# One inference step of a gMLP and S5 decoder layer: weight pairs loaded earlier in the startup, and a ring of two tiles for the last products

## The chip, the cores and the metric

The kernel runs on one core of a Trainium2 chip. The metric is device time in microseconds (us) of one execution. TensorE multiplies matrices (PE, with its weight loads as PEld), VectorE (DVE), ScalarE (ACT) and GpSimd (POOL) do the elementwise work, and SyncE (SP) issues every DMA of this kernel from one queue, in order.

## What is computed

All matrices are fp32. Besides one prompt of 2048 positions there are 8 decode positions, which run through the same matmuls as extra columns.

```python
shift, scale, gate = split(silu(c) @ w_c + b_c, 3)      # adaLN: c is 9 x 2048, w_c 2048 x 6144
h    = rmsnorm(x, g_pre) * (1 + scale) + shift          # x: 2048 x 2048 and 8 x 2048
proj = h @ w_in                                         # w_in: 2048 x 5120
u_a, v_a, z_a, x_b, z_b = split(proj)
y_a  = u_a * chunk_mix(layernorm(v_a)) * silu(z_a)      # 8 heads, chunks of 128 positions
y_b  = s5_branch(x_b) * silu(z_b)                       # 64 groups, a 64-dim complex state each
o    = concat(y_a, y_b) @ w_out                         # w_out: 2048 x 2048
out  = x + gate * rmsnorm(o, g_post)
```

## The kernel before

Activations lie transposed: 128 features on the partitions, positions along the free axis, in four blocks of 512 positions (the last has the 8 decode positions too). The contraction over 2048 features is cut into 16 K tiles of 128. Each fp32 operand is split into a high and a low part (`split`, L87: ACT casts the high part in L90, DVE or POOL subtracts it in L85 to give the low part), and one product of a weight tile and a K tile is three matmuls (`mm3`, L97 to L99). A weight load is a raw tile of 128 x 1024 fp32, 512 KB, issued by `wraw` (L106); `wpieces` turns it into two high and two low pieces.

**Startup** (`startup`, L1237; its instructions keep the order of the code on each engine). It computes the RMS statistic of block 0, the shift and scale of adaLN, and the first six column tiles of the input projection together. After the loads of x come the constants (`constants1`), whose last lines add four slices of the identity into `sel`; then 8 adaLN loads, which are a ring of 8 (`NR_`), then weight pairs of the input projection. A pair is one raw tile for two column tiles and four K tiles; there are two raw buffers for pairs. The loop over `s` runs one K tile a turn: six `kstep`s (18 matmuls) for K tile `s - 2`, four adaLN matmul groups (`ada`, L275; each frees its ring tile and issues the adaLN load 8 further on), the copy of the adaLN result (L279), its transposition through `sel` (`ada_turn`, L286), and from that h for K tile `s - 1` (`hmake`). The pairs that K tiles 4q to 4q+3 need are loaded in the turns `s = 4q` (two) and `s = 4q + 1` (the third), and split in the same two turns.

**Input projection** with everything for the S5 branch, then the **output projection** (`phase3`). In these the library orders each engine's instructions by a timeline that it plans itself: the order of the code is the priority, and an operation may be put earlier when its inputs and its tile are free. In `phase3` each block first runs four column tiles together over the 16 K tiles (six in the last block), then one column tile after the other. Each result is copied to a tile `o` (`ev_o`) and its square is added up. `final` finishes a block while the next one runs: it takes the reciprocal root R, and for each of 16 tiles multiplies `o` by R in place (L1154), adds the residual `xres` in place (L1155, POOL for even tiles and DVE for odd ones), and stores `o` (L1156). `xres` has 4 buffers, `o` has `OB` = 20. The finishing steps are called one at a time (`finish_some`) between matmuls. The last 256 positions are computed with positions on the partitions (`phase3_rows`), with weight loads from `in_woutr` and matmuls L1214 to L1216. `phase3` and `phase3_rows` load and split their first weight pairs at their start.

In `s5_mats` small results are copied from PSUM: L799 on DVE, L853 on DVE and ACT in turn.

Of the kernel before, what the change touches and what calls it, by code (L numbers as in the profile page):

```python
# [21 lines left out]
ND = 8  # L22
T = L + ND
NB = 4
# [20 lines left out]
NW = 5  # L45
OB = 20
LAG = 6
# [15 lines left out]
class Builder:  # L63
# [155 lines left out]
    def constants1(self):  # L219
        c = self.cp  # L220
        def load(name, shape):
            t = c.tile(shape, F32, name="c_" + name)
            self.SP.dma_start(t, self.I[name])
            return t
        self.ident = load("ident", [128, 128])
        self.bcT = load("bcT", [128, 48])
        self.gpre = load("gpre", [128, KT])
        self.gpost = load("gpost", [128, KT])
        self.sel = c.tile([128, 9], F32, name="sel")
        self.V.tensor_add(self.sel, self.ident[:, 0:9], self.ident[:, 32:41])  # L230
        for i in (64, 96):
            self.V.tensor_add(self.sel, self.sel, self.ident[:, i : i + 9])

# [512 lines left out]
    def s5_mats(self, pp, i):  # L746
# [51 lines left out]
        c = tl([128, 2, NQ, 32], "sc")  # L798
        V.tensor_copy(c.rearrange("p r q c -> p (r q c)"), pc[:, 0 : 2 * NQ * 32])  # L799
        dw = tl([32, NQ, 32], "dw")  # L800
# [51 lines left out]
        for g, q, jh in quarters:  # L852
            (S.copy if jh else V.tensor_copy)(kf[:, q, jh * 4 : jh * 4 + 4, :].rearrange("p j c -> p (j c)"), pk[g * 32 : g * 32 + 32, 0:128])  # L853
        V.tensor_add(kf[:, :, 0, :], kf[:, :, 0, :], dw)
# [237 lines left out]
    def phase3(self, b, ws, y):  # L1092

        V, G, SP = self.V, self.G, self.SP
        rs = ranges(b) if b < NB - 1 else ranges(b)[1:]
        c0 = rs[0][0]
        nn = rs[-1][0] + rs[-1][1] - c0
        ng = 4 if b < NB - 1 else 6
        ssq = self.xp.tile([128, TB + ND], F32, tag="ssq", bufs=2, name=self.nm("ossq"))
        kw = [{}, self.wkw]  # L1100
        ws = ws or [self.wgroup(0, 0, ng, *kw)]
        acc = [[self.ps.tile([128, 512], F32, tag="acc" if g < 4 else "aux", bufs=4, name=self.nm("acc"))] for g in range(ng)]
        os_ = []
        for k in range(KT):
            while len(y) < min(KT, k + 6):
                y.append(self.yload(b, len(y)))
            if k in (11, 13, 15):
                self.finish_some(1)
            if k % 4 == 0 and k < KT - 4:
                ws.append(self.wgroup(0, k // 4 + 1, ng, *(kw[::-1] if k // 4 % 2 == 0 else kw)))  # L1110
            for g in range(ng):
                self.kstep(acc[g], ws[k // 4][g], k, y[k], rs, k == 0, k == KT - 1)
        ynext = []
        w = self.wcol(self.I["wout"][ng])
        for g in range(ng):
            self.finish_some(1)
            os_.append(self.ev_o(b, g, acc[g], rs, ssq, G))
        for n in range(ng, 16):
            ac = [self.ps.tile([128, 512], F32, tag="acc", bufs=4, name=self.nm("acc")) for _ in rs]
            nxt = []  # L1120
            for k in range(KT):
                if k % 8 == 0 and n < 15:
                    nxt += self.wsplit(self.whalf(self.I["wout"][n + 1], k // 8), **(self.wkw if k else {}))
                self.kstep(ac, w, k, y[k], rs, k == 0, k == KT - 1)
                if k == 13:
                    self.run_later()
                if n == 15 and b < NB - 1 and k >= 4 and k % 2 == 0:
                    ynext.append(self.yload(b + 1, len(ynext)))
            self.finish_some(1 if n < 15 or b == NB - 1 else 16)
            if b == NB - 1 and n % 2 == 0 and 6 <= n < 14:  # L1130
                self.gg_rows((n - 6) // 2)
            os_.append(self.ev_o(b, n, ac, rs, ssq, G))
            w = nxt
        self.finish_some(16)
        self.finish = self.final(ssq, nn, os_, b * TB + c0, b * TB)
        return y if b == NB - 1 else ynext

    def final(self, ssq, nn, os_, t0, out0):
# [11 lines left out]
        for n in range(16):  # L1150
            if n < 13:
                load()
            o, x = os_[n][:, 0:nn], xs[n]
            V.tensor_mul(o, o, R[:, 0:nn])  # L1154
            (V if n % 2 else G).tensor_tensor(o, o, x, op=ALU.add)  # L1155
            SP.dma_start(self.O["yT"][n * 128 : n * 128 + 128, out0 : out0 + nn], o)  # L1156
            yield 1
# [13 lines left out]

    def phase3_rows(self, b, y):

        V, G, S, T, SP = self.V, self.G, self.S, self.T, self.SP
        ssq = self.sp_.tile([128, 2, 4], F32, name="ssqr")
        src = lambda i: self.I["woutr"][i // 8][:, i % 8 * 2 : i % 8 * 2 + 2, :].rearrange("p k m -> p (k m)")
        kws = [{}, self.wkw]
        ws = {i: self.wsplit(src(i), **kws[i % 2]) for i in range(4)}
        os_, xs = {}, {}
# [20 lines left out]
        for f in range(4):  # L1200
# [3 lines left out]
            for k in range(KT + lag):  # L1204
# [20 lines left out]
                if k < KT and k % 2:  # L1225
                    if i + 4 < 32:
                        ws[i + 4] = self.wsplit(src(i + 4), **kws[i % 2])
                    if f or k >= 13:
                        self.finish_some(1)
                    if f * 16 + k >= XR0 and len(xs) < 8:  # L1230
                        c, g = len(xs) // 4, len(xs) % 4
                        x = self.xp.tile([128, OW], F32, tag="o", bufs=OB, name=self.nm("xr"))[:, 0:512]
                        SP.dma_start(x, self.I["xr"][c][:, g * 512 : g * 512 + 512])
                        xs[c, g] = x


    def startup(self, st, NG, ntl):  # L1237
# [8 lines left out]
        def wraw(g, kq):  # L1246
            pair[g, kq] = self.wraw(self.wpair(I["win"], ntl[1][g], kq), st, "wraw2", 2)
        def wsplit(g, kq):
# [5 lines left out]
        for i in range(NR_):  # L1254
            raw(i)
        wraw(0, 0)
        wraw(2, 0)
        ssq = self.tile_()
        for k in range(KT):
            self.stat_add(st, xs[k], ssq, k, TB, V)  # L1260
        R = self.R[0]
        def ada(ps, i):
            self.ada_mm(ps, raws.pop(i), i % 4)
            raw(i + NR_)
# [10 lines left out]
        wsplit(0, 0)  # L1275
        wraw(4, 0)
        self.ada_ss2(0, sb)
# [9 lines left out]
        for s in range(2, KT + 2):  # L1287
# [6 lines left out]
            for q in range(NG):  # L1294
# [13 lines left out]
                if s < KT:  # L1308
                    if s % 4 == 0 and q in (0, 2):
                        wraw(q, s // 4)  # L1310
                    if s % 4 == 1 and q == 3:
                        wraw(4, s // 4)
                    if (s % 4, q) in ((0, 3), (1, 2), (1, 4)):
# [6 lines left out]
    def build(self):  # L1320
# [129 lines left out]
        self.wkw = {"pool": self.xp, "tags": ("w3h", "w3l"), "bufs": 5}  # L1450
        for b in range(NB):
            if b == NB - 1:
                self.lo_engs = [V, V, V, G]
                self.ggr = []
            y = self.phase3(b, [ws0] if b == 0 else None, y0 if b == 0 else y)
        self.phase3_rows(NB - 1, y)
        self.close(cm_x)
# [73 lines left out]
```

## Time and profile before

| | |
|---|---|
| median of three runs | 2971.8 us (2971.3 to 2975.4) |
| the profiled execution | 2969.24 us, its span 2967.4 us |
| PE busy | 2846.7 us, 96% of the span |
| DVE, ACT, POOL busy | 1590.0, 1059.7, 1046.0 us |
| mean granted TensorE clock | 0.987 of full speed |
| DMA | 581.14 MB, 196 GB/s over the span |

The profiled execution is 2.6 us below the median of the runs, and 1.8 us of it lie outside the span. Two matmuls overlap in the pipeline, so a busy PE can still run at half clock; the granted clock is told by stretch. A wait is put down to the instruction that ended it.

### The profile page before, as it was taken

The numbers are of one execution on the slowest core, as the hardware profiler recorded it, in microseconds if no ns is written. First come the engines' busy times: TensorE is split into PE (matmuls) and PEld (weight loads), VectorE is DVE, ScalarE is ACT, GpSimd is POOL, SyncE is SP. The second block draws the span as 40 slices with busy tenths as digits, with TensorE's granted clock in tenths as the row PEclk, the third lists the DMA queues.
The fourth block names the chain that finished last, engine by engine and source line by source line (L and its number), as shares of the span: only waits on it lengthen the run. The fifth ranks groups of instructions, "written<-read, shape, count | busy, mean of one in ns | idle before, by whom it ended". The sixth has DMA issues, their size and how long they took to land.

```text
span 2967.4 us, 44344 instructions
## 1 busy us (share of the span) xinstructions
PE 2846.7 (96%) x15804; PEld 2387.4 (80%) x15804; DVE 1590.0 (54%) x3026; ACT 1059.7 (36%) x1960; POOL 1046.0 (35%) x971
## 2 busy tenths in 40 slices
PE   5899899999999999999999999999999999999896
PEld 3567677777999999988888888888888878878785
DVE  4347946648543646466546745583641361543755
ACT  3224433433333232333334332433243423434442
POOL 0107735364242232323232223222324353352433
PEclk9999999999999999999999999999999999999998
DMA  8777898997887373856576566646573463564666
GB/s 299 270 201 217 237 258 236 258 270 221 194 205 214 105 232 119 251 163 189 166 215 195 161 193 185 209 132 215 162 217 110 117 206 121 142 213 128 202 199 206
DMA packets 456560, 581.14 MB, mean 196 GB/s; under 512 B 216594, under 2 KB 303122, under 8 KB 456338
## 3 DMA queue, kind: packets, MB, share of 16 engines
q1 hardware_dynamic: 456338, 578.32, 65.3%
q8 instruction: 124, 2.03, 0.3%
q14 instruction: 98, 0.79, 0.1%
HBM read 466.87 MB, written 102.66 MB: 192 GB/s over the span
## 4 chain that ended last, share of the span: by engine, by line
PE 57%; DVE 8%; DMA 3%; issue 2%; ACT 1%; SPq 0%; POOL 0%; DVEq 0%; ACTq 0%; POOLq 0%
PE acc L99 17%; PE acc L97 16%; PE acc L98 16%; DVE Ub L898 2%; DVE o L1154 1%; DVE wlo L85 1%; DMA x<-in_xT 1%; DMA wraw<-in_wout 1%; PE mix L530 1%; PE acc L1214 1%; PE acc L1215 1%; PE acc L1216 1%; DMA wraw<-in_woutr 1%; PE pg L979 1%; DVE sct L908 1%
## 5 line engine op out<-in xcount | busy, mean ns | idle before, releaser
L97 PE MATMUL acc<-hi,whi 128*128 128x512 f32 (+2 forms) x3200 | 1131.4, 355 | 4.0 <-DVE x L374 2.2
L98 PE MATMUL acc<-lo,whi 128*128 128x512 f32 (+2 forms) x3200 | 1122.3, 351 | 2.4 <-DVE lo L85 2.1
L99 PE MATMUL acc<-hi,wlo 128*128 128x512 f32 (+2 forms) x3200 | 1122.0, 351 | 1.9 <-DVE wlo L85 1.6
L85 DVE TENSOR_TENSOR wlo<-wraw,whi 128x512 fp32r<-128x512 f32 x628 | 518.9, 835 | 882.4 <-ACT whi L90 858.5
L90 ACT CAST whi<-wraw 128x512 fp32r<-128x512 f32 x960 | 581.4, 621 | 1142.7 <-PE acc L98 791.0
L85 POOL TENSOR_TENSOR wlo<-wraw,whi 128x512 fp32r<-128x512 f32 x332 | 459.8, 1387 | 1131.8 <-ACT whi L90 1027.3
L97 PEld LDWEIGHTS acc<-hi,whi 128*128 128x128 f32 x3200 | 603.2, 189 | 100.7 <-issue 23.4
L99 PEld LDWEIGHTS acc<-hi,wlo 128*128 128x128 f32 x3200 | 603.6, 189 | 90.7 <-DVE wlo L85 4.7
L98 PEld LDWEIGHTS acc<-lo,whi 128*128 128x128 f32 x3200 | 604.6, 189 | 80.2 <-DVE lo L85 3.9
L99 PE MATMUL acc<-yhi,wlo 128*128 128x512 f32 (+1 forms) x1024 | 379.6, 372 | 16.7 <-DVE wlo L85 15.2
L97 PE MATMUL acc<-yhi,whi 128*128 128x512 f32 (+1 forms) x1024 | 378.6, 370 | 6.4 <-ACT whi L90 3.6
L98 PE MATMUL acc<-ylo,whi 128*128 128x512 f32 (+1 forms) x1024 | 378.3, 370 | 0.0
L99 PEld LDWEIGHTS acc<-yhi,wlo 128*128 128x128 f32 x1024 | 195.3, 191 | 54.5 <-DVE wlo L85 18.0
L97 PEld LDWEIGHTS acc<-yhi,whi 128*128 128x128 f32 x1024 | 195.6, 191 | 42.5 <-ACT whi L90 4.1
L98 PEld LDWEIGHTS acc<-ylo,whi 128*128 128x128 f32 x1024 | 195.4, 191 | 34.0
L898 DVE SCALAR_TENSOR_TENSOR Ub<-Ub,apow 128x128 f32<-128x128 f32 (+6 forms) x384 | 143.3, 440 | 2.5 <-ACT Ub L885 2.2
L987 POOL TENSOR_TENSOR sg<-sg,zbl 128x264 f32<-128x264 f32 x64 | 54.7, 855 | 191.6 <-DVE sg L986 127.8
L1076 POOL TENSOR_TENSOR ossq<-ossq,osq 128x512 f32<-128x512 f32 (+1 forms) x60 | 81.8, 1363 | 47.8 <-ACT osq L1069 47.0
L369 ACT ACTIVATE hi<-x,shiftT 128x512 fp32r<-128x512 f32 x96 | 68.4, 724 | 82.1 <-DVE x L368 78.8
L368 DVE SCALAR_TENSOR_TENSOR x<-x,GT,R 128x512 f32<-128x512 f32 x96 | 82.2, 872 | 23.9 <-DMA x<-in_xT 23.7
L90 ACT CAST hh<-hr 128x264 fp32r<-128x264 f32 x64 | 26.4, 414 | 191.4 <-DMA hr<-Ub 107.3
L342 POOL TENSOR_TENSOR ssq<-ssq,t 128x512 f32<-128x512 f32 (+1 forms) x45 | 60.9, 1353 | 72.7 <-ACT t L341 71.8
(287 smaller groups left out, 2798.5 us busy)
## 6 DMA issues: line engine op xcount, KB each, us to landing
wraw<-in_win SPq DMA_DIRECT2D x320, 512.0 KB
wraw<-in_wout SPq DMA_DIRECT2D x128, 512.0 KB
xr<-XB SPq DMA_DIRECT2D x128, 272.0 KB
x<-in_xT SPq DMA_DIRECT2D x128, 256.0 KB
wraw<-in_wss SPq DMA_DIRECT2D x64, 512.0 KB
XB<-t SPq DMA_DIRECT2D x64, 256.0 KB
wraw<-in_wgt SPq DMA_DIRECT2D x32, 512.0 KB
MQ<-qh SPq DMA_DIRECT2D x128, 128.0 KB
```

Of the source, the lines that this page charges most:

```text
L85: eng.tensor_tensor(out, a, b, op=ALU.subtract)
L90: self.S.copy(hi, raw)
L97: mm(acc, whi, xhi, start=start, stop=False)
L98: mm(acc, whi, xlo, start=False, stop=False)
L99: mm(acc, wlo, xhi, start=False, stop=stop)
L342: add_eng.tensor_tensor(ssq[:, 0:n], ssq[:, 0:n], sq[:, 0:n], op=ALU.add)
L368: V.scalar_tensor_tensor(xt, xt, self.GT[:, k, 0:1], R[:, 0:TB], op0=ALU.mult, op1=ALU.mult)
L369: S.activation(hi[:, 0:TB], xt, AF.Identity, bias=self.shiftT[:, k, 0:1])
L530: T.matmul(pm[:, c * 128 : c * 128 + 128], self.vtok[:, c, hs], self.wsT[:, h, :], start=True, stop=True)
L898: V.scalar_tensor_tensor(o, i, f, o, op0=ALU.mult, op1=ALU.add)
L987: self.G.tensor_tensor(sg, sg, zb, op=ALU.mult)
L1076: eng.tensor_tensor(ssq[:, 0:nn], ssq[:, 0:nn], sq[:, 0:nn], op=ALU.add)
```

## The change

It moves the four-slice sum `sel` from `constants1` to after the statistic of block 0. It gives the weight pairs of the startup three buffers instead of two, issues the first three pairs together, and issues the pairs for K tiles 4q to 4q+3 in turn `s = 4q - 2` instead of `4q` and `4q + 1`. It puts the copies of L799 and L853 on ACT. In `final` the product goes into a new tile `fin` (two buffers), the sum goes into `xres`, and `xres` is stored; `OB` becomes 21. In `phase3` the finishing steps at K tiles 11, 13 and 15 come after the matmuls of that tile, and the first weight pairs of the next block (or the first two row weights) are loaded and split during the last column tile.

```diff
-OB = 20
+OB = 21
...
-        self.sel = c.tile([128, 9], F32, name="sel")
-        self.V.tensor_add(self.sel, self.ident[:, 0:9], self.ident[:, 32:41])
-        for i in (64, 96):
-            self.V.tensor_add(self.sel, self.sel, self.ident[:, i : i + 9])
...
-        V.tensor_copy(c.rearrange("p r q c -> p (r q c)"), pc[:, 0 : 2 * NQ * 32])
+        S.copy(c.rearrange("p r q c -> p (r q c)"), pc[:, 0 : 2 * NQ * 32])
...
-            (S.copy if jh else V.tensor_copy)(kf[:, q, jh * 4 : jh * 4 + 4, :].rearrange("p j c -> p (j c)"), pk[g * 32 : g * 32 + 32, 0:128])
+            S.copy(kf[:, q, jh * 4 : jh * 4 + 4, :].rearrange("p j c -> p (j c)"), pk[g * 32 : g * 32 + 32, 0:128])
...
-        ws = ws or [self.wgroup(0, 0, ng, *kw)]
+        ws = [ws]
...
-            if k in (11, 13, 15):
-                self.finish_some(1)
             if k % 4 == 0 and k < KT - 4:
                 ws.append(self.wgroup(0, k // 4 + 1, ng, *(kw[::-1] if k // 4 % 2 == 0 else kw)))
             for g in range(ng):
                 self.kstep(acc[g], ws[k // 4][g], k, y[k], rs, k == 0, k == KT - 1)
-        ynext = []
+            if k in (11, 13, 15):
+                self.finish_some(1)
+        ynext, wnext = [], []
...
-                if n == 15 and b < NB - 1 and k >= 4 and k % 2 == 0:
-                    ynext.append(self.yload(b + 1, len(ynext)))
+                if n == 15 and b < NB - 1:
+                    if k >= 4 and k % 2 == 0:
+                        ynext.append(self.yload(b + 1, len(ynext)))
+                    if k in (1, 9) or (k == 13 and b == NB - 2):
+                        g = len(wnext)
+                        wnext.extend(self.wsplit(self.wpair(self.I["wout"], g, 0), **kw[g // 4]))
+                elif n == 15 and k in (1, 9):
+                    wnext.append(self.rows_w(len(wnext)))
...
-            V.tensor_mul(o, o, R[:, 0:nn])
-            (V if n % 2 else G).tensor_tensor(o, o, x, op=ALU.add)
-            SP.dma_start(self.O["yT"][n * 128 : n * 128 + 128, out0 : out0 + nn], o)
+            t = self.xp.tile([128, TB + ND], F32, tag="fin", bufs=2, name=self.nm("fin"))[:, 0:nn]
+            V.tensor_mul(t, o, R[:, 0:nn])
+            (V if n % 2 else G).tensor_tensor(x, x, t, op=ALU.add)
+            SP.dma_start(self.O["yT"][n * 128 : n * 128 + 128, out0 : out0 + nn], x)
...
-            pair[g, kq] = self.wraw(self.wpair(I["win"], ntl[1][g], kq), st, "wraw2", 2)
+            pair[g, kq] = self.wraw(self.wpair(I["win"], ntl[1][g], kq), st, "wraw2", 3)
...
-        wraw(0, 0)
-        wraw(2, 0)
+        for g in (0, 2, 4):
+            wraw(g, 0)
         ssq = self.tile_()
         for k in range(KT):
             self.stat_add(st, xs[k], ssq, k, TB, V)
         R = self.R[0]
+        self.sel = self.cp.tile([128, 9], F32, name="sel")
+        V.tensor_add(self.sel, self.ident[:, 0:9], self.ident[:, 32:41])
+        for i in (64, 96):
+            V.tensor_add(self.sel, self.sel, self.ident[:, i : i + 9])
...
-        wraw(4, 0)
...
-                    if s % 4 == 0 and q in (0, 2):
-                        wraw(q, s // 4)
-                    if s % 4 == 1 and q == 3:
-                        wraw(4, s // 4)
+                    if s % 4 == 2 and s < KT - 4 and q % 2 == 0:
+                        wraw(q, s // 4 + 1)
```

## Rows read from the trace of the kernel before

**Rows 1.** Timeline of PE in the startup, L286 alone: start, length, instruction, idle before.
```profile
46.34 0.61 PE L286 MATMUL adat<-sel,t 128*128 128x9 f32 x4 [2.35 <-DVE t L279]
...
82.12 1.02 PE L286 MATMUL adat<-sel,t 128*128 128x9 f32 x4 [6.35 <-DVE t L279]
...
91.34 0.51 PE L286 MATMUL adat<-sel,t 128*128 128x9 f32 x4
...
98.36 0.51 PE L286 MATMUL adat<-sel,t 128*128 128x9 f32 x4
...
172.34 0.51 PE L286 MATMUL adat<-sel,t 128*128 128x9 f32 x4
```

**Rows 2.** Timeline of ACT in the startup.
```profile
29.13 1.14 ACT L90 CAST whi<-wraw 128x512 fp32r<-128x512 f32 x2 [3.46 <-DMA wraw<-in_win]
...
80.38 1.14 ACT L90 CAST whi<-wraw 128x512 fp32r<-128x512 f32 x2 [7.46 <-DMA wraw<-in_win]
```

**Rows 3.** Timeline of the SP queue in the startup.
```profile
71.42 0.38 SPq L108 DMA_DIRECT2D wraw<-in_win  x1
```

**Rows 4.** Timeline of DVE in the startup.
```profile
15.87 0.17 DVE L230 TENSOR_TENSOR sel<-c_ident 128x9 f32<-128x9 f32 x1 [11.24 <-DMA c_ident<-in_ident]
...
16.36 11.82 DVE L342 TENSOR_TENSOR t<-t,t 128x512 f32<-128x512 f32 x15
```

**Rows 5.** Waits of PE from 180 to 2190 us, its longest sum.
```profile
PE pK L850 <- POOL F L767: 6.7, 2, 3.4
```

**Rows 6.** Waits of PE from 2190 us to the end: total, times, longest.
```profile
PE acc L99 <- DVE wlo L85: 15.2, 5, 5.3
PE acc L1214 <- ACT whi L90: 8.4, 1, 8.4
PE acc L97 <- ACT whi L90: 3.6, 2, 2.6
...
PE acc L1216 <- DVE wlo L85: 1.9, 1, 1.9
```

**Rows 7.** Timeline of DVE in the output projection.
```profile
2401.04 19.02 DVE L1154 TENSOR_TENSOR o<-o,oR 128x512 f32<-128x512 f32 x15
...
2420.58 0.68 DVE L85 TENSOR_TENSOR wlo<-wraw,whi 128x512 fp32r<-128x512 f32 x1
...
2778.52 11.50 DVE L1154 TENSOR_TENSOR o<-o,oR 128x512 f32<-128x512 f32 x9
```

**Rows 8.** Stretches of the startup: busy by engine, granted clock, DMA share, GB/s.
```profile
60.00:65.00 5.00, 5.00 (x37) 3.24 (x35) 1.27 (x4) 1.43 (x2) 0.00 (x0) 1.00 1.00 322
...
100.00:105.00 5.00, 5.00 (x45) 3.11 (x35) 1.26 (x2) 1.94 (x4) 0.00 (x0) 1.00 1.02 386
...
60.00:80.00 20.00, 14.96 (x111) 9.12 (x109) 5.37 (x11) 5.16 (x8) 2.55 (x2) 1.00 0.97 334
```

**Rows 9.** Instructions on tile o, 2395 to 2450 us: ns least, median, most.
```profile
L1154 DVE TENSOR_TENSOR o<-o,oR x16: 677/1761/1792, 2401.0 to 2421.8; 128x512 f32<-128x512 f32 x16
```

**Rows 10.** Stretches of 50 us in the output projection, columns as in rows 8.
```profile
2350.00:2400.00 50.00, 50.00 (x217) 40.50 (x216) 30.31 (x35) 23.28 (x34) 13.13 (x9) 1.00 0.55 151
2400.00:2450.00 50.00, 45.43 (x190) 36.33 (x189) 41.39 (x36) 18.29 (x33) 35.50 (x22) 0.97 0.73 248
...
2600.00:2650.00 50.00, 45.42 (x191) 36.47 (x190) 27.45 (x27) 16.43 (x29) 32.13 (x21) 0.97 0.76 263
...
2750.00:2800.00 50.00, 40.20 (x268) 36.78 (x267) 40.72 (x53) 22.53 (x55) 21.08 (x16) 0.90 0.49 152
2800.00:2850.00 50.00, 45.11 (x346) 43.78 (x345) 27.39 (x40) 23.74 (x48) 23.09 (x19) 0.97 0.85 283
```

**Rows 11.** Waits of the SP queue from 2190 us: total, times, longest.
```profile
SPq L1145 <- POOL o L1155: 17.8, 8, 3.8
...
SPq L1527 <- DMA out_yr<-or: 2.2, 1, 2.2
```

**Rows 12.** The chain that ended last, 2896 to 2920 us: start, length, what.
```profile
2904.96 2.99 DMA xres<-in_xT
```

More of the change, by code (lines that the diff above doesn't have):

```diff
@@ L1135, in phase3 @@
         self.finish = self.final(ssq, nn, os_, b * TB + c0, b * TB)
-        return y if b == NB - 1 else ynext
+        return (y if b == NB - 1 else ynext), wnext
     def final(self, ssq, nn, os_, t0, out0):
@@ L1170, in gg_rows, with rows_w, phase3_rows @@
         self.later.append(turn)
-    def phase3_rows(self, b, y):
+    def rows_w(self, i):
+        return self.wsplit(self.I["woutr"][i // 8][:, i % 8 * 2 : i % 8 * 2 + 2, :].rearrange("p k m -> p (k m)"), **(self.wkw if i % 2 else {}))
+    def phase3_rows(self, b, y, ws):
         V, G, S, T, SP = self.V, self.G, self.S, self.T, self.SP
         ssq = self.sp_.tile([128, 2, 4], F32, name="ssqr")
-        src = lambda i: self.I["woutr"][i // 8][:, i % 8 * 2 : i % 8 * 2 + 2, :].rearrange("p k m -> p (k m)")
-        kws = [{}, self.wkw]
-        ws = {i: self.wsplit(src(i), **kws[i % 2]) for i in range(4)}
+        ws = dict(enumerate(ws))
+        for i in range(len(ws), 4):
+            ws[i] = self.rows_w(i)
         os_, xs = {}, {}
@@ L1226, in phase3_rows @@
                     if i + 4 < 32:
-                        ws[i + 4] = self.wsplit(src(i + 4), **kws[i % 2])
+                        ws[i + 4] = self.rows_w(i + 4)
                     if f or k >= 13:
@@ L1450, in build @@
         self.wkw = {"pool": self.xp, "tags": ("w3h", "w3l"), "bufs": 5}
[L1451 to L1456, printed above, removed]
+        y, ws = y0, ws0
+        for b in range(NB - 1):
+            y, ws = self.phase3(b, ws, y)
+        self.lo_engs = [V, V, V, G]
+        self.ggr = []
+        y, ws = self.phase3(NB - 1, ws, y)
+        self.phase3_rows(NB - 1, y, ws)
         self.close(cm_x)
```

## Prediction

> **What bounds the kernel now.** I began with the page's busy shares and clock (the table above): PE is busy nearly all the time at almost full clock, so a change can only gain where PE idles or runs at half clock. So I looked for these places, stretch by stretch, and then in the timelines of what PE waited for.
>
> In the startup the adaLN transposition L286 marks one turn of the loop. An undisturbed turn takes 98.36 - 91.34 = 7.02 us, and from the second turn's mark at 46.34 to the last at 172.34 there are 14 turns in 126.0 us [rows 1]. Undisturbed they would be 14 x 7.02 = 98.3, so 27.7 us are lost, and the loss sits at every fourth turn. The wait before 82.12 (6.35 us; two more like it follow) names a copy on DVE, but that copy stood behind a low-part subtraction, which stood behind a cast on ACT, which waited 7.46 us for a weight pair [rows 1, 2]. This third pair was issued at 71.42, within two turns of its use, behind the adaLN loads in flight, and was cast at 80.38 [rows 2, 3]. Before the loop, DVE sat 11.24 us until the identity had landed, to make `sel`, which nothing needs yet; the 15 additions of the statistic stood behind it [rows 4].
>
> From 180 to 2190 us little is lost [rows 5]. In the output projection PE waits mostly for low parts from DVE, and once 8.4 us for a weight load of the row part [rows 6]. The reader should see in the DVE timeline why: 15 products of `final` run in one piece for 19.02 us, and the low part that PE wants comes behind them, at 2420.58; at 2778.52 nine more do the same [rows 7].
>
> **The startup.** *`sel` after the statistic.* The additions take 11.82 / 15 = 0.79 us each and could begin when the first squares are there, near 6 us, so they end near 18 instead of 28.2 [rows 4]. What is late next is the first pair: it was cast at 29.13 and stays behind 16 tiles of x and 8 adaLN loads [rows 2]. From that cast the first h and its matmuls need about 4 us, so that the first marks come some 10 us earlier. I take -10; -7 if the pair lands later, -11 if the third pair, now issued beside the others, takes its wait of 2.35 us away too [rows 1]. The four small operations on `sel` cost DVE under 1 us in a place where it then waits.
>
> *Pairs two K tiles ahead.* This removes the 27.7 us [rows 1]. The new issues stand in the SP queue behind adaLN loads whose ring tiles are already free, and wait for pair buffers that were split a turn earlier, so they hold up nothing. The pairs are due in 2.4 turns or more, 17 us, against the 9 us from issue to cast that the third took [rows 2, 3].
>
> *What the queue then has to carry.* With the waits gone, a turn of 7.02 us moves four adaLN loads and on average 0.75 pairs, 4.75 x 0.524 MB = 2.49 MB, or 355 GB/s. A busy stretch of 20 us moved 334, one of 5 us as much as 386 and another 322 [rows 8]. At 334 a turn takes 7.46 us, and 12 turns with pairs give back 5.3 us; at 386 nothing, at 322 12 x 0.71 = 8.6. I take +5, since the longest busy stretch is the nearest to a stream that never stops. The Trainium skill (DMA: Bandwidth & Descriptors, "Where 436 GB/s comes from") puts the limit of one core's memory side at about 358 GB/s; by that the estimate is 2.49 / 0.358 = 6.95 us a turn and nothing given back, so the sum would be 5 us lower. The row of 386 GB/s does not fit it as a ceiling, and I go by the row of 334.
>
> Startup together: -10 - 27.7 + 5 = -32.7, between -38.7 (-11 - 27.7) and -26 (-7 - 27.7 + 8.6).
>
> **The finishing products.** In place, all products of a block can run as soon as R is there. With two `fin` tiles the third product waits until the first addition has read its tile, and that addition needs its residual. So the long piece on DVE falls apart: a weight split waits behind a few operations instead of 15. The operations are the same in number; a product takes 0.68 us at least and 1.76 in the middle while POOL adds beside it [rows 9], so DVE's work does not grow. At 2400 and 2600 us PE loses 50 - 45.43 = 4.57 and 4.58 us and 3% of 50 us, 1.5 each, to the lower clock after it [rows 10]: 12.2 in all. Behind four products, 7 us, the low part would be made near 2408 us; PE wanted it at 2420.58 + 0.68 - 4.57 = 2416.7 [rows 7, 10]. I take -11, bounds -12.2 and 0.
>
> In the last block PE loses 9.80 + 4.89 us of idle time between 2750 and 2850 and 10% + 3% of 50 us, 6.5, to the clock, 21.2 [rows 10]. The wait of 5.3 us is behind the nine products [rows 6, 7], and about 3 us of clock come with it; the rest is casts waiting for loads (3.6 us) [rows 6] and results copied late, which the ring doesn't touch. I take -8; bounds -21, if smoother finishing also brings the loads in time, and +8, if the queue below gets worse.
>
> In the row part, the waits are 1.9 us for a low part and 8.4 for a load [rows 6]: the weight load stood on SP behind residual loads and stores that waited for additions. With products paced by the ring, fewer come at once. I take -4; bounds -10.3 and +8.
>
> *What is added.* The residual's buffer is now free only when its store has landed, not when the addition is done. Each of 12 residual loads a block waits for that on SP, and behind it stand the weight loads for PE. A store was waited for 2.2 us at the end [rows 11], a residual load took 2.99 us [rows 12], an addition perhaps as long as a product beside it, 1.76 [rows 9]: 7 us around four buffers, 1.75 us a tile, 28 us a block, well inside a block's time. Up to now SP waited 17.8 us for additions in this place [rows 11]. I count nothing for it in the sum, and keep it as a rival.
>
> **At nothing.** First weights split in the last column tile, `OB` = 21, finishing steps after the matmuls: they change the order where a block begins, and there PE has no gap to lose (2350 to 2400 us is full) [rows 10]. If that cover went, each of four starts would cost up to the 9 us that a pair needs [rows 2, 3]. *Copies on ACT*: PE's longest sum of waits before 2190 us, 6.7, is for POOL [rows 5], which these copies feed. I take -1, bounds -7 and +3, since the plan's order may change with them.
>
> **Sum.** -32.7 - 11 - 8 - 4 - 1 = -56.7. From the profiled 2969.24 that is 2912.5; the median of the runs lies 2.6 higher, so 2915.
>
> **Rivals.** *Only the startup gains*: the products are spread, but their places are taken by additions that wait for residuals, with weight splits behind them as now. For it: DVE works in order and the plan's durations need not be the chip's (0.68 against 1.76 us [rows 9]). Then 2971.8 - 32.7 = 2939. Chance 0.20.
>
> *The stream is the bound*: at 322 GB/s throughout, the startup gains 29 instead of 32.7, and if its first 10 us were bound by the queue as well, 19: 2915 + 14 = 2929. Against it: the queue was idle after each wait. Chance 0.10.
>
> *All waits of the output projection go*: -38.7 - 12.2 - 21 - 10 = 2890. Chance 0.08; the late copies speak against it.
>
> *Slower*: the store's landing. If SP stands 2.2 us [rows 11] for each of 12 x 4 loads, that is 106 us of the queue; it turns the result when more than 33 us of it reach PE beyond what PE waits today, and at two thirds (70) gives 2939 + 70 - 33 = 2976 or more. The Trainium skill speaks for it (DMA: Bandwidth & Descriptors, "Latency and other measured facts"): most of the roughly 2 us fixed cost of a transfer is the wait until the target confirms the write, and memory is the slowest target. The trace agrees with its 2.2 us. Against it: a column tile of slack stands before most weight loads, and the loads can be put elsewhere in the plan. Chance 0.05; no change 0.02 (a plan that loses by accident what the startup wins).
>
> **How the numbers follow.** The forecast, 2900 to 2930 around 2915, has 0.55. The range reaches to the startup-only case and halfway to the best one: 2892 to 2946; outside lie the slower and unchanged cases and the tails. A difference under 0.2%, 6 us, can't be told from none. Faster: 0.55 + 0.20 + 0.10 + 0.08 = 0.93; same 0.02; slower 0.05.
>
> **What would show it.** Startup: statistic done near 18 us, marks of L286 each 7.0 to 7.5 us apart from about 36 us, the last near 140, no wait on `in_win`. Output projection: no piece of products longer than four on DVE, PE full across what is 2400 and 2600 us now. Wrong would be SP waiting on `out_yT` for tens of us with PE waiting for `in_wout`, or marks over 8 us apart.

## The result and the profile after

The changed kernel takes 2908.1 us (median of 4 runs, 2905.8 to 2909.8) against 2973.1 before (4 runs, 2971.3 to 2975.4): a ratio of 0.9781, 95% interval 0.9764 to 0.9797. The forecast was 2915, range 2892 to 2946. The profiled execution of the changed kernel takes 2908.74 us, its span 2906.9, 60.5 less than before; the prediction's sum was -56.7. Line numbers moved with the edits: the adaLN transposition is now L282, the product of `final` L1157, its addition L1158, its store L1159.

Five stretches show where the time came from. Their ends are the last mark of the startup (L286 before, L282 after), the first and the last start of one matmul of the S5 part (L981 before, L977 after), and the first matmul of the row part (L1214, L1221). The tile views of both kernels, before first, give least, median and longest ns, and the first and last start:

```profile
L981 PE MATMUL pg<-hh,wr x128: 278/284/288, 1046.2 to 2175.8; 128*128 128x264 f32 x128
L1214 PE MATMUL acc<-whi,yhi x128: 387/393/795, 2850.6 to 2953.0; 128*128 128x512 f32 x128
```

```profile
L977 PE MATMUL pg<-hh,wr x128: 278/284/288, 1012.0 to 2143.2; 128*128 128x264 f32 x128
L1221 PE MATMUL acc<-whi,yhi x128: 389/394/628, 2792.1 to 2894.0; 128*128 128x512 f32 x128
```

| stretch (us) | before | after | difference | forecast |
|---|---|---|---|---|
| startup, to the last mark | 172.3 | 135.9 | -36.5 | -32.7 |
| to the first L981 | 873.9 | 876.1 | +2.3 | -1 |
| to the last L981 | 1129.6 | 1131.2 | +1.6 | 0 |
| to the row part | 674.8 | 648.9 | -25.9 | -11 - 8 = -19 |
| row part, to the end of the span | 116.8 | 114.8 | -2.0 | -4 |

**Startup.** The timeline of DVE shows that the additions of the statistic now come first and `sel` behind them (two rows; before, the other way round [rows 4]). The additions end at 18.7 instead of 28.2:

```profile
8.49 10.24 DVE L338 TENSOR_TENSOR t<-t,t 128x512 f32<-128x512 f32 x13 [0.40 <-ACT t L337]
18.65 0.16 DVE L1270 TENSOR_TENSOR sel<-c_ident 128x9 f32<-128x9 f32 x1
```

The marks on PE, the counterpart of [rows 1]: the second at 37.49, and from there 14 turns in 98.37 us, 7.03 each; no stall is left.

```profile
37.49 0.61 PE L282 MATMUL adat<-sel,t 128*128 128x9 f32 x4 [1.20 <-DVE t L275]
44.62 0.51 PE L282 MATMUL adat<-sel,t 128*128 128x9 f32 x4
51.63 0.51 PE L282 MATMUL adat<-sel,t 128*128 128x9 f32 x4
...
135.86 0.51 PE L282 MATMUL adat<-sel,t 128*128 128x9 f32 x4
```

The load stream carries this. In stretches of 20 us (columns as in [rows 8]) it moves more than in any such stretch of the startup before, and from the second mark on PE is full:

```profile
20.00:40.00 20.00, 16.35 (x114) 9.31 (x107) 10.60 (x30) 5.48 (x10) 4.30 (x3) 1.00 1.03 394
40.00:60.00 20.00, 20.00 (x150) 13.04 (x154) 7.01 (x16) 4.86 (x8) 1.34 (x1) 1.00 1.02 393
60.00:80.00 20.00, 20.00 (x158) 12.83 (x158) 8.51 (x15) 6.04 (x10) 3.04 (x2) 1.00 0.98 361
...
100.00:120.00 20.00, 20.00 (x157) 12.89 (x159) 8.16 (x17) 7.42 (x12) 2.95 (x3) 1.00 0.98 353
```

**Output projection.** Where DVE ran 15 products in one piece [rows 7], it now runs one or two, and weight splits (L85) come between them:

```profile
2369.85 1.29 DVE L1157 TENSOR_TENSOR fin<-o,oR 128x512 f32<-128x512 f32 x2
2371.16 1.69 DVE L85 TENSOR_TENSOR wlo<-wraw,whi 128x512 fp32r<-128x512 f32 x1
2372.78 0.68 DVE L1158 TENSOR_TENSOR xres<-xres,fin 128x512 f32<-128x512 f32 x1
2373.38 3.49 DVE L1157 TENSOR_TENSOR fin<-o,oR 128x512 f32<-128x512 f32 x2
2376.80 1.79 DVE L85 TENSOR_TENSOR wlo<-wraw,whi 128x512 fp32r<-128x512 f32 x1
```

In this execution the products wait 9.1 us, in 9 waits, for additions of POOL to free a ring tile, which is the pacing that the prediction described. From 2190 to 2700 us PE waits for nothing. What is left stands in the last block and the row part (waits of PE from 2690 us: total, times, longest):

```profile
PE ssum L158 <- ACT sqh L90: 3.9, 1, 3.9
PE acc L97 <- DVE o L1069: 2.8, 1, 2.8
PE acc L99 <- POOL wlo L85: 1.9, 2, 1.0
```

The new wait that the slower rival spoke of is there as well. Shown are SP's waits for landed stores (same columns), and from the chain that ended last, within the row part, one such store with the residual load behind it:

```profile
SPq L1147 <- DMA out_yT<-xres: 16.9, 15, 3.5
```

```profile
2844.35 4.88 DMA out_yT<-xres
2849.29 3.14 DMA xres<-in_xT
```

### The profile page after: what moved, and what is told of

Read it like the earlier page. It is cut to its first block, busy times and chain, and to the rows that moved or that the text cites. A ratio compares the mean times of both kernels' runs of the same rounds, so it can differ in the third digit from the quotient of the medians.

```text
span 2906.9 us, 44350 instructions
## 1 busy us (share of the span) xinstructions
PE 2833.2 (97%) x15804; PEld 2377.5 (82%) x15804; DVE 1619.7 (56%) x2976; ACT 1066.7 (37%) x2008; POOL 1056.5 (36%) x973
## 4 chain that ended last, share of the span: by engine, by line
PE 77%; DVE 11%; DMA 5%; issue 3%; POOL 1%; SPq 1%; ACT 1%; DVEq 0%; ACTq 0%; POOLq 0%
PE acc L97 23%; PE acc L99 22%; PE acc L98 22%; DMA x<-in_xT 2%; DVE wlo L85 2%; DVE Ub L894 2%; PE ada L271 2%; DVE lo L366 1%; DVE x L364 1%; PE mix L526 1%; DVE sct L904 1%; DVE Ub L903 1%; DVE sct L902 1%; PE acc L1223 1%; DVE Ub L905 1%
## 5 line engine op out<-in xcount | busy, mean ns | idle before, releaser
L85 DVE TENSOR_TENSOR wlo<-wraw,whi 128x512 fp32r<-128x512 f32 x626 | 549.8, 886 | 806.2 <-ACT whi L90 788.5
L85 POOL TENSOR_TENSOR wlo<-wraw,whi 128x512 fp32r<-128x512 f32 x334 | 472.3, 1416 | 1053.6 <-ACT whi L90 955.2
L99 PEld LDWEIGHTS acc<-yhi,wlo 128*128 128x128 f32 x1024 | 193.3, 189 | 36.5 <-POOL wlo L85 2.5
L364 DVE SCALAR_TENSOR_TENSOR x<-x,GT,R 128x512 f32<-128x512 f32 x96 | 88.8, 940 | 31.1 <-DMA x<-in_xT 30.8
```

The lines of the kernel that those rows point to most:

```text
L85: eng.tensor_tensor(out, a, b, op=ALU.subtract)
L99: mm(acc, wlo, xhi, start=False, stop=stop)
L364: V.scalar_tensor_tensor(xt, xt, self.GT[:, k, 0:1], R[:, 0:TB], op0=ALU.mult, op1=ALU.mult)
```

## The experiments

All runs of one group were on one chip, with the kernel before beside them (medians 2973.0 to 2975.4). Ratios are to it.

| run | median us | ratio, 95% interval |
|---|---|---|
| e1 `sel` alone | 2970.3 | 0.9982 (0.9969 to 0.9995) |
| e2 pairs alone | 2947.4 | 0.9896 (0.9877 to 0.9914) |
| e3 both | 2937.8 | 0.9865 (0.9849 to 0.9882) |
| e4 a dead load a turn | 2915.5, one run | |
| e5 in place | 2936.6 | 0.9867 (0.9845 to 0.9888) |
| e6 late first weights | 2905.7 | 0.9767 (0.9749 to 0.9784) |
| e7 ring alone | 2942.1 | 0.9890 (0.9875 to 0.9906) |
| e8 copies back | 2907.5 | 0.9778 (0.9760 to 0.9796) |
| e9 five residual buffers | 2908.6 | 0.9789 (0.9774 to 0.9803) |
| e10 earlier finish | 2906.1 | 0.9779 (0.9763 to 0.9795) |
| e11 e6, e9 and e10 together | 2907.5 | 0.9786 (0.9771 to 0.9801) |
| e12 store from the ring | 2911.5 | 0.9788 (0.9768 to 0.9808) |

### e1 to e3: the startup's two edits, alone and together

e1 is the kernel before with the four-slice sum moved from the constants to behind the statistic:

```diff
-        self.sel = c.tile([128, 9], F32, name="sel")
-        self.V.tensor_add(self.sel, self.ident[:, 0:9], self.ident[:, 32:41])
...
         R = self.R[0]
+        self.sel = self.cp.tile([128, 9], F32, name="sel")
+        V.tensor_add(self.sel, self.ident[:, 0:9], self.ident[:, 32:41])
...
```

> The kernel before with one edit: the four-slice sum goes behind the statistic of block 0; the weight pairs stay as they were. Theory (DVE's wait for the identity holds the statistic back): the statistic ends near 18.7 us instead of 28.2, the second mark of the adaLN transposition comes 7 to 9 us earlier than 46.34, the turns that stall stay as they are, and the kernel takes about 8 us less, 2965. Rival (the first weight pair, cast at 29.13 us, is what the first matmul waits for): the statistic ends earlier all the same, but the second mark moves by less than 4 us and the time by less than 0.15%. A second rival: the queue of loads decides when the adaLN loads of the later turns land, so the earlier start is lost again at the next stalling turn, and the last mark stays within 3 us of 172.34.

e2 is the kernel before with

```diff
-        wraw(0, 0)
-        wraw(2, 0)
+        for g in (0, 2, 4):
+            wraw(g, 0)
...
-                    if s % 4 == 0 and q in (0, 2):
-                        wraw(q, s // 4)
-                    if s % 4 == 1 and q == 3:
-                        wraw(4, s // 4)
+                    if s % 4 == 2 and s < KT - 4 and q % 2 == 0:
+                        wraw(q, s // 4 + 1)
```

and three raw buffers, without the later `wraw(4, 0)`.

> The kernel before with the weight pairs alone changed: three raw buffers, the first three pairs issued together, the others two K tiles ahead; the four-slice sum stays in the constants. Theory (the stalls of every fourth turn are late pairs): the second mark stays near 46 us (44 to 46.5), after it 14 turns of 7.0 us follow, the last mark is near 144 us instead of 172.34, and the kernel takes 27 us less, 2946. Rival (the stream of loads is the bound, 334 GB/s over its busy stretches): turns with pairs take 7.4 us or more and the last mark comes after 149 us, 2951 or more.

e3 has both edits.

> The kernel before with both edits of the startup and nothing of the output projection or of the copies. Theory (the two parts add and the output projection gains by its own edits): the last mark within 1 us of the 135.86 of the changed kernel, 36 us less, 2937; the two block boundaries of the output projection still lose 4.6 us each and the last block as before. Rival (the later gain comes from another plan after an earlier start, not from the ring): part of the 26 us that the output projection gained shows up here as well, 2925 or less.

Measured: in e1 the statistic ended at 18.4 us. The first mark came at 27.95, 9.9 earlier than the 37.80 of before, the second at 39.43, 6.9 earlier, the next at 49.06, 4.4 earlier, and the last at 168.20, 4.1 earlier. The timeline of ACT in e1 says where the first 3 us stayed: the third pair, issued late as before, now holds PE up, which waits 3.04 us before the second mark.

```profile
29.94 1.14 ACT L90 CAST whi<-wraw 128x512 fp32r<-128x512 f32 x2 [13.75 <-DMA wraw<-in_win]
33.02 1.14 ACT L90 CAST whi<-wraw 128x512 fp32r<-128x512 f32 x2
37.70 1.14 ACT L90 CAST whi<-wraw 128x512 fp32r<-128x512 f32 x2 [3.54 <-DMA wraw<-in_win]
```

The turn after it took 9.63 us, against 7.13 in the changed kernel, and PE waits for nothing in it:

```profile
39.43 1.02 PE L282 MATMUL adat<-sel,t 128*128 128x9 f32 x4 [3.04 <-DVE t L275]
40.30 0.77 PE L97 MATMUL acc<-hi,whi 128*128 128x512 f32 x1
...
49.06 0.51 PE L282 MATMUL adat<-sel,t 128*128 128x9 f32 x4
```

Five of the 18 matmuls of 512 columns in this turn took 0.6 to 0.8 us, the others mostly 0.4. The same turn took 9.30, 8.66 and 9.41 us in e6, e8 and e9, which have the third pair early; in e6 the granted clock is 0.50 from 35 to 40 us. So these 2.5 us of e1 are not shown to come from the late pair.

The theory was half right. The time fell by 4.9 us, with an interval from 1.5 to 9.2 that does not exclude the 8 us; the marks do. The first rival falls, since the second mark moved by 6.9 us. The second left the last mark within 3 us of 172.34; it is missed by 1.1, less than the last marks of runs with the same startup differ (134.00 to 137.17), and most of the loss came before the third mark and not at a later stall. In e2 the marks ran on without a stall, 43.49 to 141.86, 14 turns in 98.37 us:

```profile
43.49 0.61 PE L286 MATMUL adat<-sel,t 128*128 128x9 f32 x4 [0.29 <-DVE t L279]
50.62 0.51 PE L286 MATMUL adat<-sel,t 128*128 128x9 f32 x4
...
141.86 0.51 PE L286 MATMUL adat<-sel,t 128*128 128x9 f32 x4
```

Its 2947 is near the theory's 2946, and the rival falls: the 14 turns take as long as in the changed kernel. The second mark lies 2.9 us earlier than before, so that the pairs are worth 30.5 us at the last mark and not 27.7. In e3 the last mark came at 134.33: -38.0 where the single edits sum to -4.1 - 30.5 = -34.6. So `sel` behind the statistic is worth 141.86 - 134.33 = 7.5 us beside the pairs and 4.1 alone, in one profile each, and 2.5 of the difference is the slow turn of e1. The time, 2937.8, is the 2937 expected, and the stretch from the last of the S5 matmuls to the row part is 677.5 us, no shorter than before, so the gain of the output projection is not a side effect of the earlier start.

### e4: how much the stream of loads can carry

```diff
                         wraw(q, s // 4 + 1)
+                    if 0 < s < KT and q == 3:
+                        self.wraw(self.wpair(I["win"], 6, s // 4), st, "dead", 2)
```

> The changed kernel with one more load of 512 KB in each of 15 turns of the startup loop, which nothing reads, so that a turn moves 3.01 MB on average instead of 2.49. It measures the room that the stream has. If loads come at most at the 334 GB/s of the longest busy stretch before, a turn takes 9.0 us and the last mark comes near 164; at 358 GB/s 8.4 us, near 156; at 394 GB/s, which the changed kernel shows between 20 and 60 us, 7.64 us, near 144.5; above 428 GB/s nothing changes and it stays near 136. The time follows the mark from about 2908.

The second mark came at 35.71 and the last at 137.06: 101.35 us for 14 turns, 3.0 more than in the changed kernel, for 14 loads of 512 KB more (the loop starts at `s` = 2, so there are 14 and not the 15 of the expectation). The time is that of one run; the argument rests on the marks and on the stream. The stretches of 20 us show PE nearly full:

```profile
40.00:60.00 20.00, 20.00 (x159) 12.66 (x158) 6.95 (x17) 6.00 (x10) 1.35 (x1) 1.00 1.03 401
60.00:80.00 20.00, 20.00 (x160) 12.76 (x158) 8.30 (x17) 5.28 (x9) 3.05 (x2) 1.00 1.04 400
80.00:100.00 20.00, 19.81 (x152) 12.79 (x145) 9.21 (x17) 6.43 (x11) 4.40 (x3) 1.00 1.03 404
100.00:120.00 20.00, 17.66 (x135) 10.97 (x135) 6.52 (x15) 6.85 (x12) 1.74 (x2) 1.00 1.04 401
```

The stream moves 400 to 404 GB/s for 80 us, the most that any run showed over so long. None of the cases of the expectation came: the last mark lies between the 136 of a stream above 428 GB/s and the 144.5 of one of 394. It reckoned all turns alike, but three pairs and eight adaLN loads are issued ahead of the loop, and its last two turns issue no adaLN load. By an estimate, at 400 GB/s a turn of 3.01 MB needs 7.5 us, 0.5 more than PE takes, 7 us in 14 turns. Of these 3.0 are seen, 0.4 in the turn up to 85.38 and 2.6 in the turn up to 116.02, where PE waits for adaLN loads:

```profile
PE ada L271 <- DMA wraw<-in_wss: 2.5, 3, 1.7
```

The 355 GB/s that the changed kernel's turns ask for lie well below 400.

### e5 and e7: the ring taken out, and alone

e5 is the changed kernel with this edit, and e7 the reverse edit on the kernel before:

```diff
-            t = self.xp.tile([128, TB + ND], F32, tag="fin", bufs=2, name=self.nm("fin"))[:, 0:nn]
-            V.tensor_mul(t, o, R[:, 0:nn])
-            (V if n % 2 else G).tensor_tensor(x, x, t, op=ALU.add)
-            SP.dma_start(self.O["yT"][n * 128 : n * 128 + 128, out0 : out0 + nn], x)
+            V.tensor_mul(o, o, R[:, 0:nn])
+            (V if n % 2 else G).tensor_tensor(o, o, x, op=ALU.add)
+            SP.dma_start(self.O["yT"][n * 128 : n * 128 + 128, out0 : out0 + nn], o)
```

> The changed kernel with the finishing step as before: product and addition in place in the result's tile, no ring. Everything else of the change stays. Theory (the ring is what the output projection gains): the products run again as one piece of 15 on DVE, PE loses about 4.6 us and 1.5 us of clock at each of two block boundaries and some 8 us in the last block, so the kernel takes 20 to 26 us more than the changed one, 2928 to 2934. Rival (the first weights, already split in the last column tile, or the finishing steps behind the matmuls, are what closes the gaps): 2908 to 2914.

> The kernel before with the ring of two finishing tiles alone. Theory (the ring gains by itself): 19 to 26 us less, 2949 to 2956, products in pieces of at most four, and PE without a gap at both block boundaries. Rival (the ring needs the other edits of the output projection, or the residual's buffers now wait for stores that hold weight loads back): at least 2965.

Without the ring the kernel loses 28.5 us, a little more than the 20 to 26 expected, and the stretch to the row part is 674.7 us again. DVE shows the long pieces; the low part at 2394.89 is what PE waited 4.59 us for:

```profile
2373.05 3.59 DVE L1156 TENSOR_TENSOR o<-o,oR 128x512 f32<-128x512 f32 x4
2376.57 1.78 DVE L85 TENSOR_TENSOR wlo<-wraw,whi 128x512 fp32r<-128x512 f32 x1
2378.27 14.89 DVE L1156 TENSOR_TENSOR o<-o,oR 128x512 f32<-128x512 f32 x10
2393.68 0.68 DVE L1156 TENSOR_TENSOR o<-o,oR 128x512 f32<-128x512 f32 x1
2394.89 0.68 DVE L85 TENSOR_TENSOR wlo<-wraw,whi 128x512 fp32r<-128x512 f32 x1
```

The ring alone takes 32 us off by the medians and 27.6 from profile to profile (the expectation said 19 to 26), with 649.6 us in that stretch and no more than two products in a piece. As e7 starts its output projection within 1 us of the time of before, its stretches stand beside [rows 10]; in the last two, behind both boundaries, it is some 12 us ahead:

```profile
2400.00:2450.00 50.00, 50.00 (x218) 40.47 (x217) 42.81 (x35) 17.73 (x33) 34.45 (x21) 1.00 0.74 230
2600.00:2650.00 50.00, 50.00 (x217) 40.55 (x216) 28.95 (x23) 12.83 (x23) 27.58 (x18) 1.00 0.68 210
2750.00:2800.00 50.00, 45.11 (x334) 43.18 (x333) 44.40 (x57) 25.41 (x60) 27.29 (x20) 0.93 0.66 213
2800.00:2850.00 50.00, 50.00 (x308) 44.16 (x306) 31.87 (x39) 24.89 (x52) 23.62 (x18) 1.00 0.81 258
```

At the two boundaries the whole loss is gone: 4.57 and 4.58 us of idle time and 1.5 each of clock. In the last block e7 idles 1.05 us between 2700 and 2750 too, where the kernel before has none, so idle time falls by 14.69 - 4.89 - 1.05 = 8.8 and the clock's share from 6.5 to 3.5, 11.8 in all; what the whole stretch gains beyond the boundaries is 674.8 - 649.6 - 12.2 = 13.0. The casts' waits for weight loads in the last block, 3.6 us [rows 6], are not among PE's waits in e7, and in e5 they are back with 4.0. Both rivals fall.

The ratios of e3 and e7 multiply to 0.9757, and the whole change has 0.9781. So the other edits together add nothing to startup and ring; whether they cost some us, the intervals do not tell.

### e6: the first weights not split early

```diff
-        ws = [ws]
+        ws = [ws or self.wgroup(0, 0, ng, *kw)]
...
-                    if k in (1, 9) or (k == 13 and b == NB - 2):
-                        g = len(wnext)
-                        wnext.extend(self.wsplit(self.wpair(self.I["wout"], g, 0), **kw[g // 4]))
-                elif n == 15 and k in (1, 9):
-                    wnext.append(self.rows_w(len(wnext)))
```

> The changed kernel without the early first weights: each block of the output projection and the row part load and split their first pairs at their start, as before; ring, startup and copies stay. Theory (these edits are worth nothing, since PE has no gap where a block begins): within 0.2% of the changed kernel, 2903 to 2914, and PE full at the three block starts. Rival (the cover went with the ring, because the finishing steps now hold the queue of loads longer): up to 9 us at each of four starts, 2925 or more.

2905.7 us: no change that can be measured, and PE waits for nothing from 2190 to 2700 us here too. So these edits cost and bring nothing that can be measured.

### e8: the copies back on DVE

```diff
-        S.copy(c.rearrange("p r q c -> p (r q c)"), pc[:, 0 : 2 * NQ * 32])
+        V.tensor_copy(c.rearrange("p r q c -> p (r q c)"), pc[:, 0 : 2 * NQ * 32])
...
-            S.copy(kf[:, q, jh * 4 : jh * 4 + 4, :].rearrange("p j c -> p (j c)"), pk[g * 32 : g * 32 + 32, 0:128])
+            (S.copy if jh else V.tensor_copy)(kf[:, q, jh * 4 : jh * 4 + 4, :].rearrange("p j c -> p (j c)"), pk[g * 32 : g * 32 + 32, 0:128])
```

> The changed kernel with the two PSUM copies of the S5 matrices on DVE (the second on DVE and ACT in turn) as before. From the last mark of the startup to the last of the first stage's matmuls took 873.9 us before, 872.5 with the startup's edits alone and 876.1 in the changed kernel. Theory (the copies on ACT cost 2 to 4 us there, where a gain of 1 was forecast): 2 to 4 us less, 2904 to 2906, which the stretch shows and the time hardly can. Rival (the difference is the plan's, not the copies'): no change, and the stretch stays near 876 us.

The stretch (last mark to first L981; the expectation calls its end the first stage's last matmul) took 873.7 us and the kernel 2907.5. That looked like the theory's 2 us, but the other runs with the copies on ACT gave 871.8 (e6), 873.2 (e12), 874.2 (e11), 875.9 (e10), 876.7 (e9) and 877.5 (e5) in the same stretch. In e5, e6, e9, e11 and e12 no engine's order there differs from that of the changed kernel. The copies' effect is below this scatter and stays open.

### e9 to e12: four tries at what is left

e9: `xres` with `bufs=5` and `OB = 20`. e10:

```diff
-            if k in (11, 13, 15):
+            if k in ((11, 13, 15) if b < NB - 1 else (3, 5, 7)):
                 self.finish_some(1)
...
         for g in range(ng):
-            self.finish_some(1)
+            if b < NB - 1:
+                self.finish_some(1)
```

e11 has the edits of e6, e9 and e10. e12:

```diff
-            (V if n % 2 else G).tensor_tensor(x, x, t, op=ALU.add)
-            SP.dma_start(self.O["yT"][n * 128 : n * 128 + 128, out0 : out0 + nn], x)
+            (V if n % 2 else G).tensor_tensor(t, t, x, op=ALU.add)
+            SP.dma_start(self.O["yT"][n * 128 : n * 128 + 128, out0 : out0 + nn], t)
```

> The changed kernel with five residual buffers instead of four, and 20 result tiles instead of 21 for the room. The residual's buffer is held until its store has landed; SP stood 16.9 us in 15 such waits, and in the row part one of them (a store of 4.88 us, then a load of 3.14 us) lies on the chain that ended last. Theory (this hold costs the row part the 3 us of idle time and the 1.7 us of clock near 2870): the waits for landed stores fall below 8 us and the kernel takes 3 to 5 us less, 2903 to 2905. Rival (the hold is covered; what the row part waits for are its own weight loads): SP's waits fall and the time does not, within 2 us of the changed kernel.

> The changed kernel with the finishing steps of the last block taken at K tiles 3, 5 and 7 instead of 11, 13 and 15, and none between the six evacuations that follow. In the changed kernel PE loses 4.6 us of idle time and 3.4 us of clock between 2710 and 2740 us, where the reciprocal root of R runs on DVE between the last columns' small evacuations. Theory (those evacuations stand behind the root): the gap closes to 1 us or less, 5 to 8 us less, 2900 to 2903. Rival (ACT, which waits 6.2 us for a weight load just before, is late with the evacuations whatever DVE does): the gap stays, 2906 to 2910.

> The changed kernel with five residual buffers, the earlier finishing steps of the last block, and the first weights loaded at a block's start as before. Theory (the parts add): 2897 to 2903, clearly below the changed kernel's 2908. Rival (each only moves the wait to the next late load): 2903 to 2910.

> The changed kernel with the sum put into the ring's tile and stored from there, so that the residual's buffer is free after the addition, as before, and the ring's two tiles are held until their stores have landed. Theory (what gains is that products come a few at a time, whichever tile waits for the store): 2902 to 2914, SP's waits for landed stores gone, no piece of products longer than four. Rival (two tiles held over a landing of 2 to 5 us pace the finishing so slowly that additions and stores pile up in the row part): 2916 or more, the loss in the row part.

None differs measurably from the changed kernel, so the theories of e9, e10 and e11 missed with their times. With five buffers the row part took 110.1 us instead of 114.8, what the theory said of it, and PE's wait of 3.9 for the squares' cast fell to 0.5; but the stretches before it took 6.9 more, most of it where the order is the same, and SP's waits rose instead of falling, which neither theory said:

```profile
SPq L1147 <- DMA out_yT<-xres: 24.5, 21, 3.0
```

As one profile each is all there is, whether the 4.7 us are real stays open. In e10 the gap only changed its shape. Stretches of 2700 to 2740 us, of the changed kernel and then of e10:

```profile
2700.00:2740.00 40.00, 35.37 (x257) 33.93 (x256) 27.78 (x36) 19.62 (x45) 15.49 (x13) 0.91 0.43 136
```

```profile
2700.00:2740.00 40.00, 33.91 (x248) 30.68 (x247) 39.26 (x54) 29.32 (x66) 19.89 (x14) 1.00 0.82 233
```

PE idles 6.1 us instead of 4.6 at a better clock, and DVE, now almost full, is what it mostly waits for (2.6 us for low parts of y, 1.7 for a result copied late). The wait went from one queue position to another, as e10's rival had it in effect, though not through ACT. e11 shows no sum of parts.

In e12 the products themselves wait for landed stores, which DVE's waits from 2190 us show (total, times, longest):

```profile
DVE fin L1157 <- DMA out_yT<-fin: 46.1, 29, 3.7
```

SP's waits for landed stores of `out_yT` are gone, and no piece has more than two products. The stretch to the row part took 647.2 us, the row part 120.7, 5.9 more, and PE's waits there grew for low parts (4.3 us) and casts (3.0). This profile is of the fastest of four runs (2907.3 to 2919.2). So the theory holds for the blocks of 512 columns: whichever tile waits for the store, pieces of one or two products are enough. The rival has the row part's loss right, at a smaller price than it named; the time does not show it clear of noise.

## Why the prediction was right, step by step

- **`sel` behind the statistic, -10.** Right for the first mark, which came 9.9 us earlier in e1. The second mark moved by 8.9 us (10.4 in e3), but 2.9 of it came with the pairs alone (e2): the third pair's wait, for which the prediction had allowed 1. What `sel` itself brings is 7.5 beside the pairs, near the lower bound of 7, and 4.1 without them.
- **Pairs two K tiles ahead, -27.7.** Between the marks 126.0 - 98.37 = 27.6, in e2 alone as well: right. With the wait before the second mark they bring 30.5. This term and the one of `sel` miss in opposite directions, which is luck for their sum. The prediction's reading that "the loss sits at every fourth turn" is half of it: the turn behind each stalled one is too long as well, as from 82.12 to 91.34, 9.22 us. In the three such turns (the others end at 127.85 and 165.33) PE waits for nothing and 8.3 of the 27.7 us are lost at a lower granted clock, 0.83 in this stretch of before:

```profile
80.00:100.00 20.00, 17.88 (x123) 11.28 (x127) 6.98 (x15) 4.65 (x7) 1.26 (x1) 0.83 0.62 196
```

- **The stream gives back +5.** Wrong: nothing was given back. The failed step is the choice of 334 GB/s "since the longest busy stretch is the nearest to a stream that never stops". The stream moves 393 GB/s in the changed kernel and 400 in e4; so the 334 was no limit of it. That stretch's DMA share of 0.97 did not tell so: the changed kernel has 0.98 from 100 to 120 us at 353 GB/s, about the 355 that its turns ask for. In that stretch of before SP waited 9.6 us for adaLN tiles to come free, but so it did from 40 to 60 us in the changed kernel, at 393 GB/s; the waits don't tell it either, and what kept that stretch at 334 is not shown. The 386 of a 5 us stretch was the better bound, and the rival that made the stream the limit falls.
- **Boundaries, -11.** e7 shows all 12.2 gone, the upper bound; the mechanism, short pieces with the low part between them, is the one named.
- **Last block, -8.** Mis-sized: 12 to 13 in e7. Idle time fell by 8.8 where 5.3 was counted; the casts' waits for loads went too, which the prediction had kept out of the likeliest case and put in the bound "if smoother finishing also brings the loads in time".
- **Row part, -4.** -2.0: the wait of 8.4 is gone, but the chain now goes through a store and the residual load behind it, and PE waits 3.9 for the squares' cast on ACT. Which of these sets the row part was not settled (e9).
- **Edits counted at nothing.** Right for the early weights (e6). For the copies (-1) the runs can't tell. The finishing steps behind the matmuls and `OB` = 21 had no run of their own; e7 gains what it gains without them.
- **The slower rival.** Its wait exists, at 16.9 us on SP in 15 waits, and 37.2 in 25 with the ring alone, instead of the 106 that it reckoned: 15 waits of 1.1 us on average, not 48 of 2.2. None of them left PE waiting for a load of `in_wout`. In the row part such a store does stand on the chain before loads of row weights, and PE waits 1.1 + 1.1 + 0.9 = 3.1 us there for their low parts and casts. The Trainium skill (DMA: Bandwidth & Descriptors, "Latency and other measured facts") puts most of a transfer's fixed cost of about 2 us down to the target's receipt. The waits here are of that size, 1.1 us on average and 3.5 at the longest on SP, 1.6 and 3.7 on DVE in e12; they hold the store's own transfer too, so no run here shows the receipt by itself.

Against the sum, startup (-3.8) and output projection (-6.9) came out better, row part (+2.0) and the two middle stages (+4.9) worse: together the 3.8 us between -56.7 and -60.5. The part of the two middle stages, and 1 to 2 us of the startup's, are within the scatter between profiles.

## What to carry to other kernels

When one engine runs many ready operations of low urgency in one piece, give them an output ring of two tiles whose consumer is another step of the chain: here this paced 15 products without any change to their number, and work that PE waits for came between them. A late load that stalls only every fourth turn is found by laying marks of equal turns side by side, and its whole price is the marks' excess over an undisturbed turn, that of the turn behind the stall included. Don't take a bandwidth bound from what a stretch happened to move, however busy its DMA engines look; give the stream more to carry (e4) and see what it moves. And try paired edits together, since one may hand part of its gain to the next late load.

## What the runs showed of the hardware

One core's load stream held 400 to 404 GB/s over 80 us (e4), with loads of 512 KB in one queue. The DMA share did not tell how much room was left: in the 20 us stretches named here 0.97 and 0.98 went with 334 to 361 GB/s, 1.02 to 1.04 with 393 to 404. The Trainium skill (DMA: Bandwidth & Descriptors, "Where 436 GB/s comes from") puts one core's memory side at about 358 GB/s; e4 differs, and the measurement decides. The same page ("Measured (HBM→SBUF, 128 partitions, SWDGE, issued from GpSimd)") gives 425 GB/s for a load of 16 MB with the other core of the pair idle, which these runs come near.

With every engine's instructions in the same order up to the output projection, the stretch to the first L977 took 871.8 to 877.5 us and the one from its first to its last 1130.3 to 1134.9 in six profiles (the changed kernel, e5, e6, e9, e11, e12). A difference of 5 us in one such stretch of one profile is no finding here.
